# Moving Pool's rebuilding of h, the block sums and the filler rates in a two-layer decoder trunk

## The chip, the cores and the metric

The kernel runs on one core of one Trainium2 chip. The metric is the device time of one execution in microseconds (us); lower is better. Engines are named as in the profile: PE is TensorE, DVE is VectorE, ACT is ScalarE, POOL or Pool is GpSimd, and SP is SyncE, which issues the DMAs.

## The reference

One sequence of 1024 tokens passes two layers of width 1024, all in fp32. Each layer projects the normed input to q, k, v of two attention branches and to two gates, merges the gated branches, and adds a gated convolutional FFN of inner width 2816.

```python
for l in range(DEPTH):                                   # 2
    h = rmsnorm(x, norm1[l])
    proj = h @ w_in[l]                                   # 1024 -> 5120
    qa, ka, va, qb, kb, vb, gate_pre = jnp.split(proj, splits, axis=-1)
    o_a = dilated_mixture(qa, ka, va)        # 12 heads of 64: windows 128, 512, 2048, dilation 1, 4, 16
    o_b = stick_breaking_attention(qb, kb, vb)           # 4 heads of 64
    gates = jax.nn.sigmoid(gate_pre + b_gate[l])
    merged = g_a * (o_a @ w_br[l, :OUT_A]) + g_b * (o_b @ w_br[l, OUT_A:])
    x = x + merged @ w_o[l]
    up = rmsnorm(x, norm2[l]) @ w_up[l]
    a, v = up[..., :D_FF], up[..., D_FF:]
    a = causal_depthwise_conv(a, conv_w[l], conv_b[l])   # width 3
    x = x + (jax.nn.gelu(a, approximate=False) * v) @ w_down[l]
return rmsnorm(x, norm_f)
```

## The kernel before

Every fp32 operand of a matmul is split into a high and a low part (`split`, L138 and L145: ACT casts the high part, DVE subtracts it to get the low one), and a product is three matmuls: high x high, low x high, high x low. Names ending in `_h`, `_hi` or beginning with `hh`, `oh` are high parts; `_l`, `_lo`, `hl`, `ol` low ones.

**The opening (layer 0).** `first` takes x in eight chunks of 128 tokens (`xr`). For each chunk `scaled` squares it on ACT into a buffer `xsq` to get the norm's factor (`ss`), PE transposes it (`x_t`), `kept` copies it out (`x_part`), `normed` multiplies by the factor (through PSUM, `x_rb`) into `h_raw` on DVE, and a split makes `hh` and `hl`. Chunks 0 to 2 take a shorter way, in which the squares' buffer is reused for the scaled x and no `h_raw` is kept for them. `again` (L1997) rebuilds the `h_raw` of these first 384 tokens on Pool as hh + hl, eight adds of 128x384.

Between the chunks, `head` runs the first products: v (`values_part`: `v_ps`, evicted by ACT and by DVE's `vb`, L577), k (`kq_ps`, evicted by `kq_h` L595 and `kq_l` L596) and q (`q_ps`, evicted by L592 and L593). The PSUM banks of v, k and q are shared, so that a product waits for the eviction of an earlier one. `weights` loads wk and wq; for these two (`kq_w`) Pool does both halves of the split (L167, L168).

**Block sums.** The large projections that follow run as seven products in place of eight, over 2x2 blocks of h and of the weights. `block_sums` makes the sums of h's blocks: `sum1` (L1022) and the two parts of `sum32` (L1027, L1028) on DVE, `sum4` (L1031) on Pool, and `in_two` splits each (`t_hi`, `t_lo`). They stand in a list, `todo`. Each call of `aside` does the next entry; an entry may also be `prime`, which carries the next group of seven one step on. For the weights (`in_a`) these steps are a Pool add (L1097), a DVE subtract (L1102), a Pool subtract (L1107), a DVE subtract (L1108) and the splits (`w_hi`, `w_lo`). Both layers use the same `todo`; `begin` schedules the sums' later splits by counting dense groups.

**The attention.** `attend` runs the items of a layer in a fixed order: 16 stick-breaking items (B), 4 near items (N), 16 far items (T). An item has scores and an application (`z`, `sb_t`, `sb_o` in B). Between them `dense.advance(rate)` puts in groups of six matmuls of the seven-product projections (the filler): each micro step adds the item's rate to an account, and each whole unit of it is one group. `dense.until(names)` runs filler until what an item needs is there. After the items, `dense.finish` runs the rest; then come the branch projections (`br_ps`, with weights `br_w`). The outputs of the far groups are normalised and combined through `j_ps` by DVE (L973 to L975), which gives `on`.

**What sets the order.** PE's order is the program's (`manual_schedule`). ACT, DVE and Pool are ordered by a scheduler in a simulated time, with priorities and "behind" dependencies (NO_SYNC: order on one engine only, no wait). Buffers of a tag come free in turn, and the SP queue issues its loads in order. `setup` loads the small vectors (gains, biases, taps) as five DMAs into `raw_c` at its first `next(vectors)`, and at its second turns them on PE (`pt_c`) and copies them out on DVE (L2085).

The lines that the change moves most:

```python
one = pool.tensor_tensor(RAW[0, e // 4][:, e % 4, t], hi, lo, ALU.add)
tc.add_manual_dep(one.ins, LAST["h"], SYNC, reason="after h")
```

Of the kernel before, what the change touches and what calls it, by code (L numbers as in the profile page):

```python
# [7 lines left out]
F32 = mybir.dt.float32  # L8
# [4 lines left out]
ALU = mybir.AluOpType  # L13
# [3 lines left out]
P = 128  # L17
T = 1024
D = 1024
KD = D // P  # L20
# [18 lines left out]
SYNC = mybir.DependencyInfo(mybir.DependencyClass.Sync, mybir.DependencyReason.DATA)  # L39
# [1 line left out]
IN_ORDER = {ET.PE, ET.Activation, ET.DVE, ET.Pool}  # L41
HEAD = 4
SECOND = 0.35
RATE = (1.05, 1.2, 1.3, 1.35)
RATE_N = 0.75
RATE_T = 0.62
EARLY = 5
LEAD = 6
LEAD_N = 7
# [7 lines left out]
def f32(ap):  # L57
    return ap.bitcast(F32)
# [3 lines left out]
def trunk_kernel(ctx, tc, x, norm1, w_in, b_gate, w_br, w_o, norm2, w_up, conv_w, conv_b, w_down, norm_f, out, depth=None, probe=None):  # L62
# [22 lines left out]
    LAST = {}  # L85
# [67 lines left out]
    def weights(src, cols, place=None, eng=None):  # L153

        per = 512 // cols
        got = []
        src = src.rearrange("(k p) n -> p k n", p=P)
        for r in range(0, KD, per):
            raw = sb.tile([P, per, cols], F32, tag="wr", bufs=NRAW, name="w_raw")
            nc.sync.dma_start(raw, src[:, r : r + per, :])  # L160
            if place:
                hi, lo = (x.rearrange("p (k c) -> p k c", c=cols)[:, r : r + per, :] for x in place)
            else:
                hi = sb.tile([P, per, cols], F32R, tag="wh", bufs=4, name="w_hi")
                lo = sb.tile([P, per, cols], F32R, tag="wl", bufs=4, name="w_lo")
            if eng:
                eng.tensor_copy(hi, raw)  # L167
                LAST["pool"] = pool.tensor_tensor(lo, raw, f32(hi), ALU.subtract).ins.name  # L168
            else:
                split(hi, lo, raw)  # L170
            got += [(hi[:, i, :], lo[:, i, :]) for i in range(per)]
        return got
# [829 lines left out]
            if i == 1:  # L1002
                yield

    def block_sums(dense):


        b12, b22, b11, b21 = (lambda i, n=n, k=k: RAW[n, k][:, i, :] for n in range(2) for k in range(2))

        room = {}  # L1010

        def free(t, i):
            if i % 2 == 0:
                x = sb.tile([P, 2, HF], F32, tag="p4", bufs=4, name="h_sum")
                room[t, i], room[t, i + 1] = x[:, 0, :], x[:, 1, :]
            return room[t, i]

        def behind(one, eng=1):
            tc.add_manual_dep(one.ins, LAST["head"][eng], NO_SYNC, reason="behind")

        def sum1(i):
            one = dve.tensor_tensor(free(1, i), b12(i), b11(i), ALU.subtract)  # L1022
            behind(one)
            tc.add_manual_dep(one.ins, LAST["h"], NO_SYNC, reason="behind")

        def sum32(i):
            behind(dve.tensor_tensor(free(3, i), b22(i), b12(i), ALU.subtract))  # L1027
            behind(dve.tensor_tensor(b11(i), b11(i), room[3, i], ALU.add))  # L1028

        def sum4(i):  # L1030
            pool.tensor_tensor(b21(i), b21(i), b11(i), ALU.subtract)  # L1031

        def in_two(t, i):
            if i == 0:
                if t == 4:
                    S[4] = half(0, 0)
                else:
                    new_s(t)
            src = room[t, i] if t in (1, 3) else (b11 if t == 2 else b21)(i)
            split(*S[t][i], src, "waits", LAST["head"])  # L1040

        def do(*fs):
            return set(), lambda: [f() for f in fs]

        def each(f, *args):
            return [lambda x=x: f(*x) for x in args]

        nothing = (set(), lambda: None)
        prime = lambda: dense.prime(1)
        todo = [  # L1050
            do(*each(sum1, (0,), (1,))),
            do(*each(sum1, (2,), (3,))),
            do(*each(in_two, (1, 0), (1, 1))),
            do(*each(in_two, (1, 2), (1, 3))),
            do(prime),
            do(*each(sum32, (0,))),
            do(*each(sum32, (1,))),
            do(*each(sum32, (2,))),
            nothing,
            do(*each(sum32, (3,)), *each(sum4, (0,), (1,), (2,), (3,))),  # L1060
            ({"wv"}, prime),
            do(*each(in_two, (2, 0), (2, 1))),
            nothing,
            do(*each(in_two, (2, 2), (2, 3))),
            do(prime),
            do(prime),
        ]

        def begin():
            for i in range(4):  # L1070
                dense.at(1 + i, lambda i=i: in_two(3, i))
                dense.at(6 + i, lambda i=i: in_two(4, i))

        return todo, begin
# [166 lines left out]
    def mixer(l, pending):  # L1241
# [7 lines left out]
            *((None, set(), f, True) for f in (pair_v(dense, l, 1), pair_kq(dense, l, 1, 0), pair_kq(dense, l, 2, 0))),  # L1249
            *((None, set(), f, True) for f in (pair_v(dense, l, 2), pair_kq(dense, l, 1, 1), pair_kq(dense, l, 2, 1))),  # L1250
        ]
        dense.side, dense.begin = block_sums(dense)
        dense.done |= {"K0", "K1", "V0", "V1", "V2", "V3"} | ({"wv"} if l else set())
        if l:
            next(vectors)
            units = relay(heads.pop(l)[0], primed=True)
            for i, _ in enumerate(pending):
                for _ in range(HEAD if i == 0 else i % 3 > 0):
                    next(units, None)
            dense.prime(1)  # L1260
            for _ in units:
                dense.aside()
        else:
            first_units = relay(head(l, dense))

            with tc.manual_schedule(engines={ET.Activation, ET.DVE}):
                next(pending)
                next(first_units)
                for n in (1, 2):
                    next(pending)  # L1270
                    for _ in range(n):
                        next(first_units)
            for i, _ in enumerate(pending):
                for _ in range(2):
                    next(first_units, None)
                if i == 1:
                    next(vectors)
                if i == 3:
                    dense.prime(1)
            for _ in first_units:  # L1280
                dense.aside()
        dense.done.add("head")
# [622 lines left out]
    def first():  # L1905
# [34 lines left out]
            return [tp.rearrange("p (e t) -> p e t", e=4) for tp in got]  # L1940

        def scaled(i):
            if i % 2 == 0:
                rest["pair"] = big("xsq")
            sq = rest[i] = rest["pair"][:, i % 2, :]
            ss = factor[i] = sb.tile([P, 8], F32, tag="ss", bufs=2, name="ss")
            with tc.high_priority(offset=AHEAD):
                act.activation(sq, xr[i], AF.Square, accum_out=ss[:, 0:1])
                act.activation(ss[:, 1:2], ss[:, 0:1], AF.Sqrt, bias=eps[:, 0:1], scale=1.0 / D)
                one = dve.reciprocal(ss[:, 2:3], ss[:, 1:2])  # L1950
            if i == 0:
                tc.add_manual_dep(one.ins, LAST["base"], NO_SYNC, reason="in turn")
            yield
            if i not in (3, 4, 5, 6, 7):
                for h in range(2):
                    hd = slice(h * HF, (h + 1) * HF)
                    dve.scalar_tensor_tensor(sq[:, hd], xr[i][:, hd], ss[:, 2:3], gb[h], ALU.mult, ALU.mult)
            yield
# [30 lines left out]
            for h in halves or range(2):  # L1989
                split(*(y[:, 4 * h : 4 * h + 4, c * P : (c + 1) * P] for y in H[n]), tps[i][h])  # L1990

        def again():

            t = slice(0, 3 * P)
            for e in range(KD):
                hi, lo = (f32(y[:, e, t]) for y in H[0])
                one = pool.tensor_tensor(RAW[0, e // 4][:, e % 4, t], hi, lo, ALU.add)  # L1997
                tc.add_manual_dep(one.ins, LAST["h"], SYNC, reason="after h")
            LAST["again"] = one.ins.name

        def fill(n):
# [38 lines left out]
        for i in range(1, 8):  # L2040
            load(i + 2)
            if i in (3, 4, 5, 6, 7):
                for j in {1: (0,), 2: (1,), 3: (2,)}.get(i, ()):
                    raw_t[j] = turned(xr[j], "t")
                    kept(j)
                raw_t[i] = turned(xr[i], "ts"[i % 2])
                with tc.high_priority(offset=AHEAD) if i == 3 else nullcontext():
                    kept(i)
                    normed(i)
                if i == 6:  # L2050
                    again()
                if i < 7:
                    for _ in f[i + 1]:
                        pass
            else:
                for j in {1: (0,), 2: (1,), 3: (2,)}.get(i, ()):
                    raw_t[j] = turned(xr[j], "t")
                    if j not in (0,):
                        kept(j)
                tps[i] = turned(rest[i], "s")  # L2060
                if i < 7:
                    for _ in f[i + 1]:
                        pass
                in_two(i)
                for j in {1: (0,), 2: (1,), 3: (2,)}.get(i, ()):
                    if j in (0,):
                        kept(j)
            yield
# [45 lines left out]
```

## Time and profile before

| | |
|---|---|
| runs | 2648.95 us median of 3 (2647.47 to 2650.43) |
| profiled execution | 2646.7 us, span 2644.8 us, mean granted TensorE clock 0.998 |
| PE busy | 2614.3 us (99%) |
| DVE busy | 2064.3 us (78%) |
| ACT busy | 1345.3 us (51%) |
| Pool busy | 691.4 us (26%) |

Rows of a timeline give the start, the duration, the engine, the line and the operation (out<-in, shape), how many alike stand in a row (xN), and in brackets the idle time before it and what ended that. A row of windows gives the stretch, then the busy time and number of instructions of PE, PE's weight loads, DVE, ACT and Pool, the granted TensorE clock, the share of the DMA engines and GB/s. Matmuls are pipelined, so that the start of one to the start of the next is the time one takes. The opening covers about the first 83 us of the span; layer 1's head runs over about 1320 to 1385.

### The profile page before, as it was taken

How to read it: one execution, taken by the hardware profiler on the slowest of the kernel's cores; microseconds unless marked ns; L12 is line 12 of the kernel's file. 1: busy time of each engine (PE TensorE's matmuls, PEld its weight loads, DVE VectorE, ACT ScalarE, POOL GpSimd, SP SyncE). 2: the span in 40 equal slices, each digit the busy share in tenths (PEclk: the TensorE clock that was granted, in tenths of full speed). 3: DMA queues.
4: the chain of work that ended last, by engine and by line, in shares of the span. 5: the costliest groups of instructions: out<-in, count | busy, mean ns of one | idle time of the engine just before them, and what ended most of it. 6: DMA issues, size and time to landing. Idle time of an engine off the chain costs nothing. (4 is left out here: it accounts for less than half of the span.)

```text
span 2644.8 us, 36724 instructions
## 1 busy us (share of the span) xinstructions
PE 2614.3 (99%) x12732; PEld 2183.7 (83%) x12732; DVE 2064.3 (78%) x3110; ACT 1345.3 (51%) x2500; POOL 691.4 (26%) x588
## 2 busy tenths in 40 slices
PE   9999999999999999999999999999999999999999
PEld 8788888888888888888888888888888888888887
DVE  7877767685888898896667777677858888888865
ACT  5555566574555555432445555666645455554225
POOL 4221201131244343321222211101321343334200
PEclk9999999999999999999999999999999999999999
DMA  6543487873244444688344345787632444356862
GB/s 225 159 132 120 149 218 207 214 262 88 80 148 147 160 149 154 234 318 315 143 140 143 123 134 161 197 232 206 222 97 81 165 143 160 136 175 256 335 243 113
DMA packets 400423, 468.26 MB, mean 177 GB/s; under 512 B 24309, under 2 KB 315501, under 8 KB 398445
## 3 DMA queue, kind: packets, MB, share of 16 engines
q1 hardware_dynamic: 400220, 465.90, 54.2%
q8 instruction: 101, 1.65, 0.3%
q14 instruction: 86, 0.70, 0.1%
q10 hardware_dynamic: 16, 0.00, 0.0%
HBM read 303.23 MB, written 162.59 MB: 176 GB/s over the span
## 5 line engine op out<-in xcount | busy, mean ns | idle before, releaser
L145 DVE TENSOR_TENSOR w_lo<-up_a,w_hi 128x512 fp32r<-128x512 f32 x240 | 236.8, 993 | 21.5 <-ACT w_hi L138 21.5
L138 ACT CAST w_hi<-in_a 128x512 fp32r<-128x512 f32 x252 | 156.2, 621 | 182.4 <-PE i_a L1000 50.3
L138 ACT CAST w_hi<-up_a 128x512 fp32r<-128x512 f32 x240 | 149.4, 622 | 185.1 <-PE u_a L1000 45.8
L145 DVE TENSOR_TENSOR w_lo<-in_a,w_hi 128x512 fp32r<-128x512 f32 x252 | 184.8, 735 | 58.5 <-ACT w_hi L138 52.2
L1737 DVE TENSOR_TENSOR x<-x,d_ps 128x512 f32<-128x512 f32 (+1 forms) x228 | 152.0, 672 | 78.4 <-PE d_ps L1731 77.2
L1468 POOL TENSOR_TENSOR cv<-cv 128x512 f32<-128x512 f32 x88 | 131.8, 1509 | 250.1 <-DVE cv L1463 139.9
L145 DVE TENSOR_TENSOR g<-cv,g 128x512 fp32r<-128x512 f32 x154 | 152.0, 988 | 5.2 <-ACT g L138 2.8
L1729 PE MATMUL d_ps<-gd_in,w_hi 128*128 128x512 f32 (+1 forms) x340 | 130.4, 383 | 1.6 <-ACT w_hi L138 0.8
L1731 PE MATMUL d_ps<-gd_in,w_lo 128*128 128x512 f32 (+1 forms) x340 | 129.8, 382 | 0.0
L1730 PE MATMUL d_ps<-gd_in,w_hi 128*128 128x512 f32 (+1 forms) x340 | 129.8, 382 | 0.0
L999 PE MATMUL u_a<-hh,w_hi 128*128 128x512 f32 x320 | 124.6, 389 | 1.7 <-DVE u L1619 1.6
L1000 PE MATMUL u_a<-hl,w_hi 128*128 128x512 f32 x320 | 124.5, 389 | 0.0
L1001 PE MATMUL u_a<-hh,w_lo 128*128 128x512 f32 x320 | 124.5, 389 | 0.0
L999 PE MATMUL u_a<-t_hi,w_hi 128*128 128x512 f32 x320 | 124.5, 389 | 0.0
L1000 PE MATMUL u_a<-t_lo,w_hi 128*128 128x512 f32 x320 | 124.5, 389 | 0.0
L1001 PE MATMUL u_a<-t_hi,w_lo 128*128 128x512 f32 x320 | 124.5, 389 | 0.0
L1107 POOL TENSOR_TENSOR in_a<-in_a 128x512 f32<-128x512 f32 x36 | 52.9, 1470 | 260.0 <-issue 123.2
L999 PE MATMUL i_a<-hh,w_hi 128*128 128x512 f32 x288 | 119.0, 413 | 1.3 <-DVE kq_l L596 1.3
L999 PE MATMUL i_a<-t_hi,w_hi 128*128 128x512 f32 x288 | 117.5, 408 | 0.0
L1097 POOL TENSOR_TENSOR in_a<-in_a 128x512 f32<-128x512 f32 x36 | 50.0, 1388 | 252.8 <-DMA in_a<-in_w_in_dram 142.2
L138 ACT CAST g<-cv 128x512 fp32r<-128x512 f32 x154 | 94.9, 616 | 39.5 <-POOL cv L1468 29.0
L720 DVE TENSOR_TENSOR_SCAN stay<-stay,zero 128x512 f32<-128x512 f32 (+2 forms) x96 | 93.4, 981 | 27.4 <-POOL stay L707 26.9
(384 smaller groups left out, 8449.3 us busy)
## 6 DMA issues: line engine op xcount, KB each, us to landing
gd<-g SPq DMA_DIRECT2D x154, 512.0 KB, 3.4
gd_in<-gd SPq DMA_DIRECT2D x154, 512.0 KB, 6.2
up_a<-in_w_up_dram SPq DMA_DIRECT2D x80, 512.0 KB, 5.0
in_a<-in_w_in_dram SPq DMA_DIRECT2D x72, 512.0 KB, 5.5
wd_raw<-in_w_down_dram SPq DMA_DIRECT2D x22, 1024.0 KB, 11.4
gin<-gs SPq DMA_DIRECT2D x32, 512.0 KB, 4.2
w_raw<-in_w_o_dram SPq DMA_DIRECT2D x64, 256.0 KB, 2.9
gs<-u SPq DMA_DIRECT2D x48, 256.0 KB, 5.4
```

What stands on the lines that cost most here:

```text
L138: one = act.copy(hi, src)
L145: two = dve.tensor_tensor(lo, src, f32(hi), ALU.subtract)
L720: one = dve.tensor_tensor_scan(rev, rev, zero[:, 0:1].to_broadcast([P, c1 - c0]), 1.0 if c1 == L else sv[:, c1 : c1 + 1], ALU.mult, ALU.add)
L999: pe.matmul(o, w[0][:, c], rh, start=(first and i == 0), stop=False, skip_group_check=True)
L1000: pe.matmul(o, w[0][:, c], rl, start=False, stop=False, skip_group_check=True)
L1001: pe.matmul(o, w[1][:, c], rh, start=False, stop=(last and i == 3), skip_group_check=True)
L1107: pool.tensor_tensor(a21, a22, a11, ALU.subtract)
L1468: return lambda: pool.tensor_tensor(dst, a, b, ALU.subtract)
L1729: pe.matmul(o[:, sub], wh[:, c], gh[:, sub], start=(i == 0 and k in (0, 4, 5)), stop=False, skip_group_check=True)
L1730: pe.matmul(o[:, sub], wh[:, c], gl[:, sub], start=False, stop=False, skip_group_check=True)
L1731: pe.matmul(o[:, sub], wl[:, c], gh[:, sub], start=False, stop=(i == m - 1), skip_group_check=True)
L1737: dve.tensor_tensor(x, x, o[:, sub], ALU.add)
```

## The change

1. `again` is split into two groups of four Pool adds. The first is placed on Pool behind wk's second low part, the second behind wq's, with order dependencies in place of a wait for the last split of h; it is called at chunks 4 and 5 instead of 6.
2. The squares of chunks 4 to 7, which nothing reads, go to buffers of the tag "ot" instead of the tag that wk's weights share.
3. In layer 0 `next(vectors)` is called after the chunks instead of at the second one.
4. The four `sum4` leave the list and go to `begin`, each just before the split that reads it.
5. Layer 1 gets a list of its own, in which the first group's `prime` steps come later and stand among the `sum32` entries, and the first two `in_two` come after those.
6. The rates fall: RATE by 0.02 to 0.03, RATE_T from 0.62 to 0.58. RATE_N stays.

```diff
--- before.py
+++ after.py
@@ -41,9 +41,9 @@
 IN_ORDER = {ET.PE, ET.Activation, ET.DVE, ET.Pool}
 HEAD = 4
 SECOND = 0.35
-RATE = (1.05, 1.2, 1.3, 1.35)
+RATE = (1.03, 1.17, 1.27, 1.32)
 RATE_N = 0.75
-RATE_T = 0.62
+RATE_T = 0.58
 EARLY = 5
 LEAD = 6
 LEAD_N = 7
@@ -165,7 +165,7 @@
                 lo = sb.tile([P, per, cols], F32R, tag="wl", bufs=4, name="w_lo")
             if eng:
                 eng.tensor_copy(hi, raw)
-                LAST["pool"] = pool.tensor_tensor(lo, raw, f32(hi), ALU.subtract).ins.name
+                LAST.setdefault("pools", []).append(pool.tensor_tensor(lo, raw, f32(hi), ALU.subtract).ins.name)
             else:
                 split(hi, lo, raw)
             got += [(hi[:, i, :], lo[:, i, :]) for i in range(per)]
@@ -1002,7 +1002,7 @@
             if i == 1:
                 yield
 
-    def block_sums(dense):
+    def block_sums(dense, l):
 
 
         b12, b22, b11, b21 = (lambda i, n=n, k=k: RAW[n, k][:, i, :] for n in range(2) for k in range(2))
@@ -1045,30 +1045,52 @@
         def each(f, *args):
             return [lambda x=x: f(*x) for x in args]
 
-        nothing = (set(), lambda: None)
+        nothing = do()
         prime = lambda: dense.prime(1)
-        todo = [
-            do(*each(sum1, (0,), (1,))),
-            do(*each(sum1, (2,), (3,))),
-            do(*each(in_two, (1, 0), (1, 1))),
-            do(*each(in_two, (1, 2), (1, 3))),
-            do(prime),
-            do(*each(sum32, (0,))),
-            do(*each(sum32, (1,))),
-            do(*each(sum32, (2,))),
-            nothing,
-            do(*each(sum32, (3,)), *each(sum4, (0,), (1,), (2,), (3,))),
-            ({"wv"}, prime),
-            do(*each(in_two, (2, 0), (2, 1))),
-            nothing,
-            do(*each(in_two, (2, 2), (2, 3))),
-            do(prime),
-            do(prime),
-        ]
+        if l:
+            todo = [
+                do(*each(sum1, (0,), (1,))),
+                do(*each(sum1, (2,), (3,))),
+                nothing,
+                do(*each(sum32, (0,))),
+                do(*each(sum32, (1,))),
+                do(*each(sum32, (2,))),
+                do(prime),
+                nothing,
+                do(*each(sum32, (3,))),
+                do(*each(in_two, (1, 0), (1, 1))),
+                do(*each(in_two, (1, 2), (1, 3))),
+                nothing,
+                do(prime),
+                do(*each(in_two, (2, 0), (2, 1))),
+                do(prime),
+                nothing,
+                do(*each(in_two, (2, 2), (2, 3))),
+                do(prime),
+            ]
+        else:
+            todo = [
+                do(*each(sum1, (0,), (1,))),
+                do(*each(sum1, (2,), (3,))),
+                do(*each(in_two, (1, 0), (1, 1))),
+                do(*each(in_two, (1, 2), (1, 3))),
+                do(prime),
+                do(*each(sum32, (0,))),
+                do(*each(sum32, (1,))),
+                do(*each(sum32, (2,))),
+                nothing,
+                do(*each(sum32, (3,))),
+                ({"wv"}, prime),
+                do(*each(in_two, (2, 0), (2, 1))),
+                nothing,
+                do(*each(in_two, (2, 2), (2, 3))),
+                do(prime),
+                do(prime),
+            ]
 
         def begin():
             for i in range(4):
-                dense.at(1 + i, lambda i=i: in_two(3, i))
+                dense.at(1 + i, lambda i=i: (sum4(i), in_two(3, i)))
                 dense.at(6 + i, lambda i=i: in_two(4, i))
 
         return todo, begin
@@ -1249,7 +1271,7 @@
             *((None, set(), f, True) for f in (pair_v(dense, l, 1), pair_kq(dense, l, 1, 0), pair_kq(dense, l, 2, 0))),
             *((None, set(), f, True) for f in (pair_v(dense, l, 2), pair_kq(dense, l, 1, 1), pair_kq(dense, l, 2, 1))),
         ]
-        dense.side, dense.begin = block_sums(dense)
+        dense.side, dense.begin = block_sums(dense, l)
         dense.done |= {"K0", "K1", "V0", "V1", "V2", "V3"} | ({"wv"} if l else set())
         if l:
             next(vectors)
@@ -1273,10 +1295,9 @@
             for i, _ in enumerate(pending):
                 for _ in range(2):
                     next(first_units, None)
-                if i == 1:
-                    next(vectors)
                 if i == 3:
                     dense.prime(1)
+            next(vectors)
             for _ in first_units:
                 dense.aside()
         dense.done.add("head")
@@ -1940,9 +1961,9 @@
             return [tp.rearrange("p (e t) -> p e t", e=4) for tp in got]
 
         def scaled(i):
-            if i % 2 == 0:
+            if i in (0, 2):
                 rest["pair"] = big("xsq")
-            sq = rest[i] = rest["pair"][:, i % 2, :]
+            sq = rest[i] = rest["pair"][:, i % 2, :] if i < 4 else sb.tile([P, T], F32, tag="ot", name="xsq")
             ss = factor[i] = sb.tile([P, 8], F32, tag="ss", bufs=2, name="ss")
             with tc.high_priority(offset=AHEAD):
                 act.activation(sq, xr[i], AF.Square, accum_out=ss[:, 0:1])
@@ -1989,13 +2010,13 @@
             for h in halves or range(2):
                 split(*(y[:, 4 * h : 4 * h + 4, c * P : (c + 1) * P] for y in H[n]), tps[i][h])
 
-        def again():
+        def again(k):
 
             t = slice(0, 3 * P)
-            for e in range(KD):
+            for e in range(4 * k, 4 * k + 4):
                 hi, lo = (f32(y[:, e, t]) for y in H[0])
-                one = pool.tensor_tensor(RAW[0, e // 4][:, e % 4, t], hi, lo, ALU.add)
-                tc.add_manual_dep(one.ins, LAST["h"], SYNC, reason="after h")
+                one = pool.tensor_tensor(RAW[0, k][:, e - 4 * k, t], hi, lo, ALU.add)
+                tc.add_manual_dep(one.ins, LAST["pools"][1 + 2 * k], NO_SYNC, reason="behind")
             LAST["again"] = one.ins.name
 
         def fill(n):
@@ -2047,8 +2068,8 @@
                 with tc.high_priority(offset=AHEAD) if i == 3 else nullcontext():
                     kept(i)
                     normed(i)
-                if i == 6:
-                    again()
+                if i in (4, 5):
+                    again(i - 4)
                 if i < 7:
                     for _ in f[i + 1]:
                         pass
```

## The prediction

> **What bounds the kernel now.** I read the page first, then TensorE's waits, then the timelines around the longest ones.
>
> ```profile
> PE 2614.3 (99%) x12732; PEld 2183.7 (83%) x12732; DVE 2064.3 (78%) x3110; ACT 1345.3 (51%) x2500; POOL 691.4 (26%) x588
> ```
>
> TensorE (PE) is busy 2614.3 of 2644.8 us. The change keeps every matmul, and the transposes that it moves in the opening are the same ones. So the only time to win is in PE's roughly 30 us of idle time, and in matmuls that run slowly just after it. The list of PE's waits says where that is:
>
> ```profile
> PE v_ps L179 <- DVE kq_l L596: 3.8, 1, 3.8
> PE kq_ps L179 <- DVE vb L577: 2.6, 1, 2.6
> PE br_ps L179 <- DVE on L974: 2.3, 2, 1.1
> PE v_t L1196 <- DVE vv L1202: 2.2, 4, 1.1
> PE i_a L999 <- DVE kq_l L596: 1.3, 1, 1.3
> PE x_rb L1978 <- DVE h_raw L1982: 0.7, 1, 0.7
> ```
>
> The columns are the total, the count and the longest. The kq_ps, i_a and x_rb waits lie in the opening, v_ps in the head of layer 1, br_ps once in each layer, and v_t in the attention. All but v_t end on a DVE instruction whose place the change alters. A wait also costs something after it ends:
>
> ```profile
> 53.98 0.28 PE L181 MATMUL v_ps<-w_hi,hl 128*128 128x256 f32 x1
> 56.86 0.68 PE L179 MATMUL kq_ps<-hh,kq_w 128*128 128x512 f32 x1 [2.60 <-DVE vb L577]
> 57.34 0.63 PE L180 MATMUL kq_ps<-hl,kq_w 128*128 128x512 f32 x1
> 57.76 0.63 PE L181 MATMUL kq_ps<-hh,kq_w 128*128 128x512 f32 x1
> ...
> 1358.82 0.39 PE L181 MATMUL q_ps<-hh,kq_w 128*128 128x512 f32 x1
> 1363.01 0.39 PE L179 MATMUL v_ps<-v_w,hh 128*128 128x256 f32 x1 [3.81 <-DVE kq_l L596]
> ...
> 1359.00:1363.00 4.00, 0.20 (x1) 0.00 (x0) 2.05 (x5) 3.18 (x6) 1.82 (x1) 1.00 0.00 0
> 1363.00:1367.00 4.00, 3.99 (x23) 3.99 (x24) 3.96 (x7) 2.42 (x5) 0.23 (x1) 0.66 0.58 215
> 1367.00:1371.00 4.00, 4.00 (x33) 4.00 (x32) 3.78 (x5) 0.81 (x2) 1.43 (x1) 0.91 0.40 133
> ```
>
> After the wait at 53.98 the 512-column matmuls start 0.42 us apart (57.34 to 57.76). The rows at 549.13 and 549.36 below show the usual 0.23. Nine go that slowly, and 9 x 0.2 = 1.8 us is lost. After the wait at 1358.82 the granted clock of a 4 us window falls to 0.66, then 0.91: 4 x 0.34 + 4 x 0.09 = 1.7 us lost. The 1.3 us wait for i_a is followed by nothing of the kind.
>
> **The opening.** What bounds it from 45 us on is DVE's queue, not PE:
>
> ```profile
> 45.56 1.46 DVE L145 TENSOR_TENSOR hl<-h_raw,hh 128x512 fp32r<-128x512 f32 x1
> 46.95 5.77 DVE L1022 TENSOR_TENSOR h_sum<-h_raw 128x512 f32<-128x512 f32 x4
> 52.64 3.56 DVE L145 TENSOR_TENSOR t_lo<-h_sum,t_hi 128x512 fp32r<-128x512 f32 x4
> 56.12 0.68 DVE L577 TENSOR_TENSOR vb<-v_ps,vb 128x512 fp32r<-128x512 f32 x1
> 56.73 1.28 DVE L1027 TENSOR_TENSOR h_sum<-h_raw 128x512 f32<-128x512 f32 x2
> 60.81 1.78 DVE L145 TENSOR_TENSOR w_lo<-in_a,w_hi 128x512 fp32r<-128x512 f32 x1
> 63.72 0.68 DVE L577 TENSOR_TENSOR vb<-v_ps,vb 128x512 fp32r<-128x512 f32 x1
> 71.41 0.68 DVE L596 TENSOR_TENSOR kq_l<-kq_ps,kq_h 128x512 fp32r<-128x512 f32 x1
> ...
> 42.07 10.10 POOL L1997 TENSOR_TENSOR h_raw<-hh,hl 128x384 f32<-128x384 f32 x8 [8.02 <-DVE hl L145]
> 53.26 1.80 POOL L1097 TENSOR_TENSOR in_a<-in_a 128x512 f32<-128x512 f32 x1
> ```
>
> A two-operand DVE instruction takes 0.64 us (L1027, 1.28 for two) with Pool quiet, but 1.44 (L1022, 5.77 for four) while Pool runs the eight adds of L1997. Pool stood idle for 8.02 us before them. The change does four of them behind wk's splits, once chunk 2 of h is split, and four behind wq's. By the order of the changed kernel all eight are done before the last hl.
>
> - The hl at 45.56 falls from 1.46 to 0.68, and the four sums from 5.77 to 2.56: 0.78 + 3.21 = 4.0 us. With some further shortening of the t_lo group, which can gain at most 3.56 - 2.56 = 1.0 us where L1097 no longer runs beside it, I take 4.2. The vb that ends at 56.80 then ends at 52.6.
> - PE reaches kq_ps at 54.1 now (53.98 and one more 0.12 us step) and some 0.7 earlier without the x_rb wait, so at 53.4. The 2.6 us wait and its slow matmuls go, with a margin of 0.8.
> - From that vb to the next DVE now needs 64.40 - 56.80 = 7.6 us. The change puts one more w_lo into that stretch, 0.68 to 1.78 us. I take 1.78, since Pool's sum4 still runs there. 52.6 + 7.6 + 1.8 = 62.0, 2.4 earlier than now.
> - PE, through with kq_ps at 53.4 + 24 x 0.23 = 58.9, now waits for that vb: a new wait of 3.1 us before q_ps, probably with slow matmuls behind it. It doesn't cost the end: 62.0 + 24 x 0.23 + 1.8 = 69.3, ahead of what follows.
> - From there to the end of kq_l (72.09 now) is 7.7 us, with one w_lo fewer but in_a's subtract behind Pool's sum4: unchanged, 69.7. So i_a starts 2.3 us earlier.
>
> I take -2.3 us. If w_lo and Pool collide worse, -0.5 is left; if DVE kept up with PE everywhere, all of 2.6 + 1.8 + 1.3 + 0.7 = 6.4 would go.
>
> The rest of the opening I take at nothing. Squares moved to other buffers let wk's weights and the last chunks come sooner: at most the x_rb wait, counted above. The five small vector loads leave SP's queue ahead of x's chunks and come some 30 us later; their first reader is a transpose just before the copies of L2085 at 73.8, so unless their landing slips by over 25 us they cost nothing. What SP issues behind them, the first in_a loads, also comes sooner than now.
>
> **The head of layer 1.** Now ACT stands idle, and kq_h queues behind a weight cast and four t_hi casts:
>
> ```profile
> 1359.06 0.62 ACT L138 CAST w_hi<-in_a 128x512 fp32r<-128x512 f32 x1 [7.16 <-DVE in_a L1108]
> 1359.58 2.17 ACT L138 CAST t_hi<-h_sum 128x512 fp32r<-128x512 f32 x4
> 1361.66 0.57 ACT L595 CAST kq_h<-kq_ps 128x512 fp32r<-128x512 f32 x1
> ...
> 1357.25 1.77 DVE L1108 TENSOR_TENSOR in_a<-in_a 128x512 f32<-128x512 f32 x1
> 1362.27 0.69 DVE L596 TENSOR_TENSOR kq_l<-kq_ps,kq_h 128x512 fp32r<-128x512 f32 x1 [1.87 <-ACT kq_h L595]
> ...
> 1355.11 3.37 POOL L1031 TENSOR_TENSOR h_raw<-h_raw 128x512 f32<-128x512 f32 x2 [1.83 <-DVE h_raw L1028]
> 1359.70 1.82 POOL L1031 TENSOR_TENSOR h_raw<-h_raw 128x512 f32<-128x512 f32 x1 [1.23 <-DVE h_raw L1028]
> ```
>
> The change takes kq_h out from behind those casts. In exchange kq_l now stands, on DVE, behind in_a's second subtract, which waits for a Pool subtract queued behind three sum4. Those take 1.7 us each (3.37 for two). The first one's operand now comes early, since one L1027 and L1028 pair moved ahead of in_a's first subtract; the other two are free from about 1354.9 (1355.11 now) and run back to back to 1358.3. The Pool subtract then ends near 1360.1, in_a's within 1 us of that at 1361.1, and kq_l's at 1361.7. v_ps starts at 1361.8 in place of 1363.01: -1.2 us. A wait of 3 us is left, so I leave the 1.7 us of slow clock in. Bounds: 0, if Pool is one instruction later, and 3.8 + 1.7 = 5.5 if kq_l comes free of Pool.
>
> [...]
>
> **Before br_ps, both layers.**
>
> ```profile
> 549.13 0.39 PE L1000 MATMUL i_a<-hl,w_hi 128*128 128x512 f32 x1
> 549.36 0.40 PE L1001 MATMUL i_a<-hh,w_lo 128*128 128x512 f32 x1
> 553.14 0.50 PE L179 MATMUL br_ps<-oh_b,br_w 128*128 128x512 f32 x1 [1.14 <-DVE on L974]
> ...
> 552.01 1.08 DVE L974 TENSOR_TENSOR on<-on,j_ps 128x512 f32<-128x512 f32 x1
> ```
>
> PE waits until L974 has read the second j_ps. With the lower rates more dense matmuls are left over at the end, and by the changed order six stand between that j_ps and br_ps: 6 x 0.23 = 1.4 us, more than the 1.14. They come out of the attention, where they covered something else (below). L974 also moves ahead of a split that waits for ACT. So -1.1 in each layer, -2.2 together; bounds 0 and -2.3 (the whole wait).
>
> **Attention, lower rates.** Per layer the far items keep 288 dense matmuls of 300, and the stick-breaking ones get 840 for 834. At three group boundaries of each layer the next item's scores are no longer laid under the item before; 18 or 24 dense matmuls go ahead of them instead. The work is the same; the cost is what PE waits when a chain isn't covered. The nearest case is the first item, which starts in that very way now:
>
> ```profile
> 89.50 0.28 PE L637 MATMUL z<-kv,slots 128*128 128x128 f32 x1
> 92.40 0.49 PE L732 MATMUL sb_t<-ident,beta 128*128 128x128 f32 x3
> ...
> 440.00:500.00 60.00, 60.00 (x365) 52.70 (x364) 44.44 (x104) 35.46 (x84) 9.24 (x9) 1.00 0.89 227
> ```
>
> From its last score to the first use of the result it is 2.9 us, and PE filled them without a wait. DVE is busy 44 of 60 us late in the attention, so it isn't the bound there. I take 0; between -1 (one of the v_t waits gone) and +2.9 for each boundary left bare.
>
> **Sum.** -2.3 - 1.2 - 2.2 = -5.7 us, between -0.5 and -14.2 with the attention at 0. The profiled execution took 2646.7 (2644.8 span and 1.9 around it), so 2641.0; it stands 2.25 below the median of the runs, 2648.95, which gives 2643.2 as a median.
>
> **Rivals.**
> - *The waits only move* (0.13). The opening keeps 0.5 of its gain because the new q_ps wait and its slow matmuls reach i_a; layer 1 gains nothing because kq_l waits for Pool where it waited for ACT. For: both new queue places are in the order. 0.5 + 2.2 = 2.7: 2646.2.
> - *DVE gets free of Pool* (0.22). Both head waits vanish with their slow matmuls: 6.4 + 5.5 + 2.3 = 14.2: 2634.7. [...] Against: 3 us of DVE work still stand between PE and its next bank in the opening.
> - *Slower: the bare boundaries* (0.15). At the two stick-breaking boundaries of each layer the chain of 2.9 us is uncovered, because the dense matmuls that should cover it were used up ahead of the scores. 4 x 2.9 = 11.6, less 5.7: +5.9, 2654.9. It turns the sign from 1.4 us a boundary on. Against: the first item, same form, without a wait.
> - *Nothing but noise* (0.05): each gain is taken back by the next wait on DVE, 2649. That the edits don't take hold is excluded by the order.
>
> The forecast keeps 0.45. Faster or slower by 0.2% means 5.3 us, about what a measurement here can tell from no change; -5.7 is just past it, so of the forecast's 0.45 I count 0.27 as faster and 0.18 as the same. Faster: 0.27 + 0.22 + 0.02 of the first rival = 0.51. Slower: 0.15 and 0.02 of the last = 0.17. The same: 0.32. The range, 2636 to 2653, leaves out the far half of the second rival and the far end of the third.
>
> **What would show it.** Right: the adds of `again` near 20 to 25 and 34 to 39 us, DVE's four L1022 at 0.64 each, no kq_ps wait, a q_ps wait of about 3 us behind vb, i_a near 69.8; v_ps in layer 1 about 1.2 us sooner behind kq_l, its releaser in turn a Pool subtract; no br_ps wait. Wrong: DVE's instructions as long as before; the granted clock low over a longer stretch of the opening; new PE waits for z, sb_t or sb_o at the boundaries; or more v_t waits.

## The result, and the profile after

The changed kernel takes 2661.8 us (median of 5 runs, 2658.66 to 2663.19) against 2648.95 (here of 5 runs, 2647.47 to 2654.62): it is slower, by a ratio of 1.0042 (95% interval 1.0027 to 1.0057). The forecast was 2643.2, the range 2636 to 2653.

The profiled execution has a span of 2657.0 us, 12.2 more than before. PE's waits, in the columns known from before:

```profile
PE sb_t L732 <- DVE beta L724: 8.0, 6, 2.6
PE i_a L999 <- DVE kq_l L596: 3.1, 1, 3.1
PE v_t L1218 <- DVE vv L1224: 2.3, 3, 1.6
...
PE br_ps L179 <- DVE on L974: 2.2, 2, 1.3
PE v_ps L179 <- DVE kq_l L596: 2.0, 1, 2.0
```

The kq_ps wait of the opening is gone and the v_ps wait is half as long. But br_ps waits as before, i_a waits 3.1 us where it waited 1.3, and the waits for `beta`, in the stick-breaking items, have grown from 0.3 us in all to 8.0.

To see where the time went, take two marks of each layer: the start of the first score `z` and that of the first `br_ps`. Between them lies the attention with its 1464 filler matmuls, the same number in both kernels. The rows are the answers on the two tiles, before and then after, layer 0 and then layer 1; "a to b" are the first and the last start.

```profile
L636 PE MATMUL z<-kv,slots x80: 220/326/500, 83.6 to 412.9; 128*128 128x256 f32 x36, 128*128 128x512 f32 x24, 128*128 128x128 f32 x12, 128*128 128x384 f32 x8
L179 PE MATMUL br_ps<-oh_b,br_w x32: 389/389/501, 550.4 to 594.8; 128*128 128x512 f32 x32
L636 PE MATMUL z<-kv,slots x80: 220/326/500, 1387.8 to 1717.8; 128*128 128x256 f32 x36, 128*128 128x512 f32 x24, 128*128 128x128 f32 x12, 128*128 128x384 f32 x8
L179 PE MATMUL br_ps<-oh_b,br_w x32: 389/389/500, 1855.3 to 1899.7; 128*128 128x512 f32 x32
```

```profile
L636 PE MATMUL z<-kv,slots x74: 220/330/500, 82.3 to 413.2; 128*128 128x256 f32 x30, 128*128 128x512 f32 x24, 128*128 128x128 f32 x12, 128*128 128x384 f32 x8
L179 PE MATMUL br_ps<-oh_b,br_w x30: 389/389/470, 557.3 to 598.5; 128*128 128x512 f32 x30
L636 PE MATMUL z<-kv,slots x72: 220/330/497, 1392.7 to 1705.9; 128*128 128x256 f32 x29, 128*128 128x512 f32 x24, 128*128 128x128 f32 x11, 128*128 128x384 f32 x8
L179 PE MATMUL br_ps<-oh_b,br_w x32: 387/389/467, 1866.7 to 1911.1; 128*128 128x512 f32 x32
```

| stretch | before | after | difference |
|---|---|---|---|
| start to the first z (the opening) | 83.6 | 82.3 | -1.3 |
| attention of layer 0 | 466.8 | 475.0 | +8.2 |
| to layer 1's first z | 837.4 | 835.4 | -2.0 |
| attention of layer 1 | 467.5 | 474.0 | +6.5 |
| to the end | 789.5 | 790.3 | +0.8 |

The opening and the stretch with the head of layer 1 gain 3.3 us; the attention loses 14.7.

**A boundary in the attention.** The rows are PE's, DVE's and Pool's at the second boundary of layer 0, and then windows with the granted clock:

```profile
214.70 0.40 PE L637 MATMUL z<-kv,slots 128*128 128x512 f32 x1
219.38 0.30 PE L732 MATMUL sb_t<-ident,beta 128*128 128x128 f32 x1 [0.67 <-DVE beta L724]
222.21 0.69 PE L732 MATMUL sb_t<-ident,beta 128*128 128x128 f32 x2 [2.53 <-DVE beta L724]
...
216.76 1.29 DVE L720 TENSOR_TENSOR_SCAN stay<-stay,zero 128x512 f32<-128x512 f32 x1 [4.83 <-POOL stay L707]
221.47 0.68 DVE L724 TENSOR_TENSOR beta<-beta,stay 128x512 f32<-128x512 f32 x1
...
213.69 1.29 POOL L1119 TENSOR_TENSOR in_a<-in_a 128x512 f32<-128x512 f32 x1 [16.97 <-DMA in_a<-in_w_in_dram]
214.93 1.31 POOL L1129 TENSOR_TENSOR in_a<-in_a 128x512 f32<-128x512 f32 x1
216.17 0.31 POOL L707 TENSOR_SCALAR_AFFINE_SELECT beta<-beta 128x128 f32<-128x128 f32 x1
...
219.00:223.00 4.00, 1.09 (x4) 0.93 (x5) 3.15 (x5) 0.45 (x2) 0.00 (x0) 0.75 0.60 197
223.00:227.00 4.00, 4.00 (x13) 3.12 (x13) 3.14 (x5) 1.52 (x3) 0.00 (x0) 0.50 0.00 0
```

The item before is through, so PE has run 24 dense matmuls, and the scores `z` start only at 211.81. The item has two pairs of scores; the first row is the last of them. (A third group of z stands at 216.32 to 217.00. It has the 512 and 128 columns of the next item, whose first scores `attend` puts ahead of this item's sb_t, and the waiting sb_t doesn't need it.) The scores need their mask on Pool (L707), which stands there behind two steps for a weight; DVE has nothing to do for 4.83 us until the mask is there, and then has a u add, a weight split and an in_a subtract among the two scans. So the chain, from the item's last score to the end of the last beta that its first sb_t needs (222.15), is 7.5 us long. PE has 12 dense matmuls (two groups of six) and that third z for this time, waits 0.67 and 2.53 us, and then runs 4 us at a clock of 0.50.

### The profile page after: what moved, and what is told of

Same layout as the page of the kernel before. It is cut to its first block, busy times and chain, and to the rows that moved or that the text cites. A ratio compares the mean times of both kernels' runs of the same rounds, so it can differ in the third digit from the quotient of the medians.

```text
span 2657.0 us, 36747 instructions
## 1 busy us (share of the span) xinstructions
PE 2617.5 (99%) x12732; PEld 2187.5 (82%) x12732; DVE 2068.4 (78%) x3110; ACT 1348.3 (51%) x2500; POOL 691.0 (26%) x588
## 4 chain that ended last, share of the span: by engine, by line
PE 81%; DVE 10%; issue 3%; DMA 3%; ACT 2%; SPq 1%; POOL 0%; DVEq 0%; ACTq 0%; POOLq 0%
PE u_a L999 5%; PE u_a L1001 5%; PE u_a L1000 5%; PE d_ps L1750 5%; PE d_ps L1751 4%; PE d_ps L1752 4%; PE i_a L999 4%; PE i_a L1000 4%; PE i_a L1001 4%; PE u_c L999 3%; PE u_c L1001 3%; PE u_c L1000 3%; PE o_ps L179 2%; PE o_ps L180 2%; PE o_ps L181 2%
## 5 line engine op out<-in xcount | busy, mean ns | idle before, releaser
L1119 POOL TENSOR_TENSOR in_a<-in_a 128x512 f32<-128x512 f32 x36 | 49.6, 1378 | 291.2 <-DMA in_a<-in_w_in_dram 137.6
L1001 PE MATMUL i_a<-hh,w_lo 128*128 128x512 f32 x288 | 114.8, 399 | 0.0
L1000 PE MATMUL i_a<-hl,w_hi 128*128 128x512 f32 x288 | 114.5, 398 | 0.0
```

Source lines behind the costliest of these rows:

```text
L1000: pe.matmul(o, w[0][:, c], rl, start=False, stop=False, skip_group_check=True)
L1001: pe.matmul(o, w[1][:, c], rh, start=False, stop=(last and i == 3), skip_group_check=True)
```

## Experiments

All times are medians, with the ratio to the kernel before and its 95% interval. "A group" is six filler matmuls.

**Run 1: the old rate in the changed kernel.** `RATE = (1.05, 1.2, 1.3, 1.35)`, all else as in the change.

> The changed kernel with RATE, the rate of the stick-breaking items alone, set back to (1.05, 1.2, 1.3, 1.35). By its order the scores of the next group again lie under the item before, at all boundaries. Theory A (the boundaries left bare cost 3.5, 7.3, 3.6 and 4.4 us in the two layers): 18.8 us less than the changed kernel, 2643, and below the kernel before. Rival B (the new opening or layer 1's new list upset what follows, the rate does not matter): 2658 or more. Rival C (less filler per item is what costs, wherever the scores lie): 2643 as well, told apart by the third run.

2645.07 us, 0.9983 (0.9974 to 0.9991). 16.7 us of the change's time hang on these four numbers. The attention takes 468.3 and 469.8 us, and no wait before br_ps is left.

**Run 2: the low rate alone.** The kernel before with `RATE = (1.03, 1.17, 1.27, 1.32)`.

> The kernel before with only RATE lowered to (1.03, 1.17, 1.27, 1.32). Its order shows the same bare boundaries as the changed kernel. Theory A: 2649 + 18 = 2667, with sb_t waits for beta of 2 to 3 us after the bare boundaries. Rival B: 2649, since opening and list are as before.

2663.55 us, 1.0059 (1.0046 to 1.0071); the attention takes 475.6 and 474.6. The rate does it without the rest of the change: rival B falls.

**Run 3: a shorter lead.** The changed kernel with

```diff
-LEAD = 6
+LEAD = 5
```

> The changed kernel with its low rates and LEAD 5 in place of 6: a fetched row counts as there after five groups of filler instead of six, and by the order no stick-breaking boundary is bare any more. Theory A: 2643 to 2645, the waits for beta gone, perhaps a short wait for a DMA. Rival C: still near 2661, as the filler per item is as low.

2663.37 us, 1.0053 (1.0040 to 1.0066). The long waits for beta at the boundaries are gone, and nothing is won: the attention takes 477.8 and 477.1 us. The lead also sets when far items' fetches count as there, and far scores now wait 5.5 us for their DMA (t_kq); v_t waits 4.2 us for vv.

**Run 4: the far items' rate alone.** The kernel before with `RATE_T = 0.58`.

> The kernel before with only RATE_T lowered from 0.62 to 0.58. Theory A: the boundaries stay covered, so within 2 us of 2649; the wait before br_ps (1.14 us a layer) goes if six more matmuls stand ahead of it. Rival C: 3 us or more slower, as the far items have 12 matmuls less per layer.

2647.14 us, 0.9993 (0.9984 to 1.0002): no loss; the br_ps wait is gone. Two groups, not one, are left over ahead of br_ps here.

**Run 5: the shorter lead for the stick-breaking rows alone.** The changed kernel with

```diff
-self.at(LEAD, lambda j=self.b: self.done.add(f"FB{j}"))
+self.at(LEAD - 1, lambda j=self.b: self.done.add(f"FB{j}"))
```

> The changed kernel with its low rates; only the row fetches of the stick-breaking groups count as there after five groups of filler instead of six, the fetches of the far items keep their own lead (run 3 changed those too). By the order no boundary inside the stick-breaking items is bare. Theory A (bare boundaries): 2645, as with the old rate. Rival C (less filler as such): 2660.

2657.15 us, 1.0037 (1.0024 to 1.0051). Neither theory: with no bare boundary 4.7 us of the median come back of 16.7, and in the profiled execution the attention is no shorter (475.4 and 477.4 us against 475.0 and 474.0). The waits for beta fall from 8.0 to 1.6 us, those for t_kq rise to 7.1 (0.7 in the changed kernel), those for vv to 3.8.

**Run 6: the rate half way.** The changed kernel with `RATE = (1.04, 1.185, 1.285, 1.335)`.

> The changed kernel with RATE half way back, (1.04, 1.185, 1.285, 1.335). By its order the row fetches are there in time and no boundary inside the stick-breaking items is bare. Theory A, a step: all of the loss gone, 2645. Rival C, a loss in proportion to the rate: half of it, 2653.

2666.3 us, 1.0070 (1.0058 to 1.0083): worse than either end, which neither a step nor a proportion allows. Waits on other producers take the place of those for beta: v_t waits 11.4 us for vv, and the far scores 3.3 us for t_kq.

Theory A as I had put it, that a bare boundary is what costs, falls with runs 5 and 6. So I looked at what stands at each boundary. In the kernel before, the first item, which I had taken for the same case, has two groups right ahead of its first sb_t (three behind its own last score). The changed kernel's second boundary has one (two behind its last score). This became theory A2.

The first item of layer 1 shows the price of such a group by itself. In the kernel before 12 dense matmuls stand right ahead of its sb_t, in the changed kernel 6; the chain is 5.7 us long in both. The rows of before, then after:

```profile
1396.55 0.44 PE L732 MATMUL sb_t<-ident,beta 128*128 128x128 f32 x2 [0.28 <-DVE beta L724]
```

```profile
1401.37 0.44 PE L732 MATMUL sb_t<-ident,beta 128*128 128x128 f32 x2 [1.69 <-DVE beta L724]
```

The wait grows by 1.4 us, and six matmuls at 0.23 us are 1.4 us. Run 2 has it as well (1.64), run 1 hasn't (0.33).

**Run 9: bare boundaries at the old rate.** The kernel before with `LEAD + 1` in the line of run 5.

> The kernel before, old rates, opening and list, but the row fetches of the stick-breaking groups count as there after seven groups of filler instead of six. By the order the three boundaries inside the stick-breaking items of each layer become bare, and at each of them twelve dense matmuls stand right before the first sb_t, as ahead of the first item before. In the changed kernel the second boundary has six there and lost 5.9 and 2.7 us; the first has twelve and lost about 1. Theory A (each bare boundary costs 3.5 to 7): 2649 + 6 x 4.7 = 2677. Theory A2 (it costs only where six stand before the first sb_t in place of twelve): about 1 us each, 2655 or less, and no wait for beta over 1.5 us.

2664.95 us, 1.0061 (1.0048 to 1.0073). A is wrong: the boundaries are bare, and PE's waits in the stick-breaking items of layer 0, of which the first fence has the longest, have no beta in them (nor have those of layer 1). A2 had said so, yet the total is 10 us above its figure. The second fence has the longest waits in the far items of layer 0, where the kernel before waits only for br_ps (1.1):

```profile
PE v_t L1196 <- DVE vv L1202: 2.2, 3, 1.0
PE i_a L999 <- DVE u L1148: 0.8, 1, 0.8
```

```profile
PE z L636 <- DMA t_kq<-tk: 2.2, 2, 1.5
PE o L916 <- DVE p1l L145: 1.9, 3, 0.9
```

A bare boundary draws filler forward, 18 matmuls in a row ahead of its scores, and the far items miss it: from the last `o` of the near items to the first br_ps 300 filler matmuls lie in layer 0, 342 in the kernel before. The run doesn't isolate A2 either: at its second boundary Pool is done with the same two weight steps 2.0 us before the masks, and beta ends 3.7 us after the last score.

**Run 10: one group more.** The changed kernel, at a bare stick-breaking boundary:

```diff
                     dense.advance(rate)
+                if alone and name[0] == "B" and items[i + 1][0][0] == "B":
+                    dense.step()
```

> The changed kernel with one more group of six dense matmuls after the scores of a bare stick-breaking boundary; rates low as in the change. Theory A2: the waits of 2.5 us for beta at the second boundary and the slow clock after them go, 6 to 8 us over both layers: 2654 to 2656. Theory A (bare as such): 2661.

2655.28 us, 1.0022 (1.0012 to 1.0032): 6.5 us less than the changed kernel by the medians, as A2 said. From 150 to 240 us PE waits 3.2 us for beta in the changed kernel. The rows are PE's only wait in that stretch here, then the second boundary of layer 0 (in this kernel L735 is the sb_t, L727 the beta and L710 the mask) and a window behind it:

```profile
PE i_a L1002 <- ACT u L1143: 0.2, 1, 0.2
...
216.45 0.40 PE L640 MATMUL z<-kv,slots 128*128 128x512 f32 x1
221.47 0.49 PE L735 MATMUL sb_t<-ident,beta 128*128 128x128 f32 x3
...
219.62 0.69 DVE L727 TENSOR_TENSOR beta<-beta,stay 128x512 f32<-128x512 f32 x1
...
214.88 0.38 POOL L710 TENSOR_SCALAR_AFFINE_SELECT beta<-beta 128x128 f32<-128x128 f32 x1 [0.33 <-ACT beta L706]
...
222.00:226.00 4.00, 4.00 (x21) 3.26 (x20) 3.34 (x5) 2.69 (x6) 0.00 (x0) 1.00 0.00 0
```

The wait and the half clock behind it are both gone. But that isn't shown to be the group's doing alone. Six matmuls cover 1.4 us, and the two waits were 3.2. Pool's order has moved too: its two weight steps are done before the mask (Pool is idle for 0.33 us before it), nothing stands among the scans, and from the last score (216.45) to the end of beta (220.31) it is 3.9 us in place of 7.5. No run holds Pool's order fixed and adds the group.

Nor do the traces place the 6.5 us: the attention takes 472.2 us in layer 0 (475.0 in the changed kernel) but 476.4 in layer 1 (474.0), where the wait at the second boundary is gone as well but v_t waits 3.6 us in place of 1.6. The two profiled executions differ by 2.8 us only.

**Runs 7 and 8: the opening alone, the list alone.** The kernel before with the first three edits of the change; the kernel before with layer 1's list.

> The kernel before with the opening's three edits alone (the two groups of again, the squares' buffers, the vectors' loads); rates and list as before. From the traces of the changed kernel and of run 1, where the first sb_o comes 2.3 and 1.7 us sooner: 2647, 2 us less. If the opening's gain were larger and lost later: 2645.

> The kernel before with layer 1's own list alone, its sum4 moved with it; opening and rates as before. By run 1, in which the head of layer 1 gained 1.2 to 1.7 us: 2647.5. If the wait only moves from ACT to Pool: 2649.

The opening: 2649.06 us, 1.0001 (0.9992 to 1.0009), no gain; the first z comes 0.8 us sooner though i_a starts 3.3 sooner. The list: 2645.33 us, 0.9990 (0.9981 to 0.9998).

**Runs 12 and 13: PE kept busy in the opening.** Run 7 with matmuls added in front of the first i_a, 44 and then 10:

```diff
             pe.transpose(pt[:, at[i] : at[i + 1]], raw[:n, i, :], ident[:n, :n])
+        for _ in range(0 if l else 10):
+            pe.matmul(pt[:, 2 * P : 3 * P], ident, ident, start=True, stop=True)
```

> The kernel before with the opening's three edits and, in the wait of 3.3 us before the first i_a, 44 idle matmuls of 128 columns on PE whose result nobody reads (only added work). Theory S (the opening's gain of 3.3 us at i_a is eaten by matmuls at half clock after the long wait): the clock stays up, i_a starts as early as in run 7 and its matmuls run at full speed, 2 us less than run 7: 2647. If the gain is lost elsewhere: 2649.

> As run 12, but with 10 idle matmuls in place of 44: in run 12 each of them took two passes of 0.115 us, 10.1 us in all, so the stretch ran 7 us past the wait of 3.3 us; the clock did stay at 1.00 and i_a then ran at 0.23 us a matmul. Ten take 2.3 us and end just as i_a comes free at 68.8. Theory S (half clock after the wait eats the gain): 2 us less than run 7 (2649.1), so 2647. If the loss of run 7 lies elsewhere: 2649.

Run 12: 2654.96 us, 1.0023 (1.0013 to 1.0033); the added work ran past the wait. Run 13: 2645.72 us, 0.9986 (0.9977 to 0.9995), 3.3 less than run 7. The first fence has a window of run 7 behind its wait, the second run 13's rows and window:

```profile
70.00:74.00 4.00, 4.00 (x11) 3.13 (x10) 4.00 (x11) 2.08 (x5) 0.00 (x0) 0.50 0.69 203
```

```profile
65.64 2.50 PE L2084 MATMUL pt_c<-ident 128*128 128x128 f32 x20
68.83 0.50 PE L999 MATMUL i_a<-hh,w_hi 128*128 128x512 f32 x1 [0.69 <-DVE kq_l L596]
...
70.00:74.00 4.00, 4.00 (x20) 3.27 (x19) 4.00 (x12) 4.00 (x8) 0.00 (x0) 1.00 0.65 198
```

i_a starts at 68.8 in both. With PE idle before it, the granted clock is 0.50 from 70 to 74 us and PE starts 11 matmuls there; with PE busy it is 1.00 and PE starts 20. Added work that computes nothing makes the kernel faster. Theory S stands for the opening: the first z comes 1.4 us sooner than in run 7 (81.4 against 82.8). The rest of the 3.3 us isn't placed.

**Runs 11 and 14: the parts that gain.** The list with `RATE_T = 0.58`; and these with the opening and run 13's ten matmuls. RATE is the old one in both.

> The kernel before with layer 1's list and RATE_T 0.58, the opening and RATE as before. If the gains of the two edits alone add up (3.3 and 1.6 us by their medians): 2644, the fastest so far; if they overlap: 2645.5.

> The kernel before with layer 1's list, RATE_T 0.58, the opening's three edits and the ten idle matmuls of run 13; RATE as before. If the gains add up (run 11: 5.1 us, run 13: 2): 2642. If the opening's gain is lost again: 2644, as run 11.

Run 11: 2643.76 us, 0.9981 (0.9972 to 0.9989). Run 14: 2641.80 us, 0.9971 (0.9960 to 0.9983), the fastest of all, 7.9 us below the kernel before beside it (2649.71).

## Why the prediction was wrong

**The step that failed is "Attention, lower rates": taken as 0, measured as +14.7 us** (8.2 and 6.5). Runs 1 and 2 put it on RATE: with the old rate 16.7 us come back, with the low one alone the kernel before loses 14.8 of its median. What misled me was the precedent, and I had misread it. I took 2.9 us, from the row at 89.50 to the first sb_t, as the first item's chain. That row is a score of the next item (128 columns); the first item's own last score is this one, with its mask and its beta:

```profile
87.38 0.39 PE L637 MATMUL z<-kv,slots 128*128 128x512 f32 x1
...
90.20 0.69 DVE L724 TENSOR_TENSOR beta<-beta,stay 128x512 f32<-128x512 f32 x1
...
85.81 0.29 POOL L707 TENSOR_SCALAR_AFFINE_SELECT beta<-beta 128x128 f32<-128x128 f32 x1 [1.91 <-ACT beta L703]
```

So its chain is 3.5 us (87.38 to 90.89), and PE had 5.0 us of work to lay over it, up to 92.40. At the second boundary of the changed kernel both sides differ: the chain is 7.5 us, with Pool's two weight steps ahead of the masks and three other DVE instructions among the scans, and PE has one group less. Waits of 3.2 us, and in layer 1 of 2.9, are left there, in layer 0 with 4 us at a clock of 0.50 behind them. Where the groups stand could be read from the changed order beforehand; the sum had priced neither side.

**The third rival came nearest; its size and its sum were off.** 2654.9 was forecast. It priced four boundaries at 2.9 us each, 11.6 together, by the same misread row; the second boundary of each layer waited, the first didn't wait for beta. The attention lost 14.7, and of the 5.7 us of gains set against it 2.5 came (the other three rows of the table). I gave it 0.15, on the strength of the precedent.

How the 14.7 us are made up is shown only in part. That the low rate costs them is shown both ways (runs 1 and 2). One group less is worth 1.4 us of wait where the chain is as long as before (first item of layer 1). How much of the waits at the second boundaries is the missing group, and how much Pool's place in the chain, stays open: no run separates them. In all four waits of over 2.5 us (the changed kernel and run 2, both layers) Pool's two weight steps stand directly ahead of the masks; in runs 9 and 10 they end before the masks are due or just then, and PE doesn't wait. Runs 3, 5 and 6 show that without bare boundaries the attention loses as much or more elsewhere in the profiled executions, at v_t (which waits for vv) and at the far scores (which wait for t_kq). Run 9 shows that filler drawn forward is missed by the far items. That the old rates just happen to place the groups where no such wait arises fits all runs, but no run isolates it.

**Opening: -2.3 forecast, -1.3 measured at the first z.** The first steps of the working hold. The adds run where they were said to (first row below at 20 us, second at 34), DVE's four sums take 0.64 us each except the two beside Pool's in_a add (2.39 together), and the vb at 51.48 ends at 52.15 (52.6 forecast):

```profile
19.98 3.92 POOL L2018 TENSOR_TENSOR h_raw<-hh,hl 128x384 f32<-128x384 f32 x4 [2.45 <-DVE hl L145]
33.67 4.84 POOL L2018 TENSOR_TENSOR h_raw<-hh,hl 128x384 f32<-128x384 f32 x4
45.19 1.60 POOL L1119 TENSOR_TENSOR in_a<-in_a 128x512 f32<-128x512 f32 x1 [5.67 <-DMA in_a<-in_w_in_dram]
54.09 8.03 POOL L1031 TENSOR_TENSOR h_raw<-h_raw 128x512 f32<-128x512 f32 x3 [7.30 <-ACT w_hi L138]
...
44.95 2.39 DVE L1022 TENSOR_TENSOR h_sum<-h_raw 128x512 f32<-128x512 f32 x2
47.87 1.28 DVE L1022 TENSOR_TENSOR h_sum<-h_raw 128x512 f32<-128x512 f32 x2
51.48 0.67 DVE L577 TENSOR_TENSOR vb<-v_ps,vb 128x512 fp32r<-128x512 f32 x1
57.49 0.67 DVE L577 TENSOR_TENSOR vb<-v_ps,vb 128x512 fp32r<-128x512 f32 x1
59.19 1.78 DVE L145 TENSOR_TENSOR w_lo<-in_a,w_hi 128x512 fp32r<-128x512 f32 x1
62.59 3.46 DVE L145 TENSOR_TENSOR t_lo<-h_raw,t_hi 128x512 fp32r<-128x512 f32 x2
67.94 0.69 DVE L596 TENSOR_TENSOR kq_l<-kq_ps,kq_h 128x512 fp32r<-128x512 f32 x1
```

From one vb to the next I had set 9.4 us, with Pool in the way. It took 6.0 (52.15 to 58.16): nothing there stretched. So no wait before q_ps appeared. The DVE instructions that took longer beside Pool's came behind that vb: w_lo (1.78; 0.67 at 56.89, though Pool's first sum4, 4.63 us long, runs there too) and t_lo (3.46 for two; 1.28 for two at 68.54, Pool's last add having ended at 65.50). All the waiting gathered before i_a, 3.1 us. There the half clock that I had placed behind q_ps, hidden, stands on the path (0.50 in the 4 us from 68.68). i_a starts 3.5 us sooner, 68.68 for 72.15, and 2.2 of that are lost again by the first z (in run 7, 2.5 of 3.3). Run 13 shows why: with the clock kept up (1.00 from 66 to 78 us) the first z comes 2.2 us sooner than before.

**Head of layer 1: -1.2 forecast, -2.0 measured for the whole stretch up to layer 1's first z.** v_ps waits 2.0 us in place of 3.8, the releaser is the one named, and the slow clock stays, as forecast (0.59 from 1368 to 1372):

```profile
1364.71 1.73 POOL L1129 TENSOR_TENSOR in_a<-in_a 128x512 f32<-128x512 f32 x1
...
1366.47 0.69 DVE L1130 TENSOR_TENSOR in_a<-in_a 128x512 f32<-128x512 f32 x1 [1.17 <-POOL in_a L1129]
1367.08 0.68 DVE L596 TENSOR_TENSOR kq_l<-kq_ps,kq_h 128x512 fp32r<-128x512 f32 x1
...
1368.00:1372.00 4.00, 4.00 (x22) 4.00 (x23) 3.97 (x6) 1.45 (x3) 1.66 (x1) 0.59 0.36 124
```

**br_ps: -2.2 forecast, 0 measured.** The six matmuls do stand ahead of br_ps. But DVE's L974 moved as well: an i_b add of the filler, two splits of br_w, L975 and L973 now stand between the second j_ps and it (before: L975 and a split), and it ends 3.4 us after the second j_ps (2.5 before). Filler isn't only cover for PE; each group sends work to DVE, and I had counted only PE's side. Runs 1 and 4, with two groups left over, do lose the wait.

## What to carry to other kernels

Where filler is dealt out by a rate, a small change of the rate changes which groups stand between which steps, and the loss isn't in proportion to it. So compare in the new order, at each place and not by totals, how many matmuls lie between a producer's last input and its first use, and what stands in the queues of the engines between them; a precedent holds only if both are the same. To name a chain's last input, follow the tile that the wait names: here the nearest row of the same line belonged to the next item. A wait that is shortened or moved should be priced with the clock that follows it: in the opening the waits gathered into one of 3.1 us (in the changed kernel and in run 7), the clock behind it was 0.50 and most of the gain was lost there, and idle matmuls in that wait won it back (2649.1 to 2645.7 us by the medians, 1.4 us of it seen in the opening).

## What the runs showed of the hardware

In these runs the granted clock did not follow from the length of a wait alone. Behind PE waits of 2.0 us (layer 1's head after, 0.59 from 1368 to 1372), 2.5 (after, at 222.21, then 0.50 in the next 4 us), 2.6 (before, 53.98 to 56.86, then 0.57) and 3.1 us (after, i_a at 68.68, then 0.50) it fell; behind the 1.3 us wait for i_a before (72.15) it stayed at 1.00. But behind a gap of 2.9 us at 1533.11 in the changed kernel, where `sb_t` waited 2.6 us for beta in layer 1, it stayed full:

```profile
1533.00:1537.00 4.00, 3.89 (x20) 3.27 (x21) 2.96 (x5) 1.96 (x4) 0.00 (x0) 1.00 0.16 57
```

What sets this gap apart from the one at 222.21, 2.8 us from start to start, isn't shown.

The fp32 matmuls of 128 columns against the identity that were added in the opening showed as two matmul records each, of about 0.115 us: run 12's 44 as 88, which took 10.09 us.
